# A second buffer for the gates' tile of two SwiGLU FFNs, with a smaller scratch for dynamic transfers

## The chip, the core and the metric

The kernel runs on one core of one Trainium2 chip. A core has a matrix engine (TensorE, PE in the profile; PEld is its loading of weights), three engines for elementwise work (VectorE or DVE, ScalarE or ACT, GpSimd or POOL) and SyncE (SP), which here only issues transfers. Operands lie in on-chip memory of 128 partitions (SBUF); TensorE writes its results to a second, small memory (PSUM), from where VectorE and ScalarE fetch them. Each engine has a list of instructions of its own and waits on semaphores for the others. The metric is the device time of one execution in microseconds (us).

## The reference, cut to what matters

Two layers of a transformer-like network work on 512 latent and 256 context tokens with a model width of 1024, in float32. Each layer has a mixer (attention and linear recurrences) and then an FFN:

```
def _swiglu(h, w_gate, w_up, w_down):
    return (jax.nn.silu(h @ w_gate) * (h @ w_up)) @ w_down
...
x_lat = x_lat + m_lat[5] * _rms(_swiglu(h_lat, ffn_w_gate[l], ffn_w_up[l], ffn_w_down[l]), norm_post_ffn[l])
```

The inner width is 2816, or 22 chunks of 128. Layer 0 (FFN 0) has 768 tokens, layer 1 (FFN 1) the 512 latent ones. The factors `m_lat` come from a product of a conditioning vector with `mod_w`, 6144 columns per layer.

## The kernel before, in words

Each float32 operand is split into a high part (H) and a low part (L) that TensorE multiplies fast, and a product is the sum of three matmuls HH, HL, LH. A weight block comes by a transfer on SP's queue into `raw` (three buffers); ScalarE copies its high part to `wH`, VectorE subtracts to get `wL` (L672 and L673 for whole units, L727 and L728 for the pairs below).

`ffn` works on the 22 chunks in pairs. For each pair it makes a *gate unit* (`product(wg, c0, "go", todo)`) and an *up unit* (`product(wu, c0, "uo")`), and between and behind them adds a part of the result of `w_down` (`acc_part`, PSUM tiles `acc`, sums into `y` on VectorE, L820). The first pair is done apart (`first`), so each FFN has ten gate units and ten up units with `product`.

A unit multiplies a 2 × 2 block matrix of weights with one of activations by Strassen's scheme, in `seven`: seven block products of 12 matmuls each instead of eight. With n = 384 (FFN 0) or 256 (FFN 1) columns per matmul, the blocks are, in program order, `11` (PSUM tile `ab`, first half), `U1` (`E`), `12` (`ab`, second half), `U2` (`ab`, first half again), `22` (`D`), `S4` (`E`) and `V` (`ab`). This text calls `22` block D, `U1` block E where it follows `11`, and keeps the names 11, 12, U2, V. In the rows of the profile and of the instruction lists, 11 is `ab<-b`, 12 is `ab<-x` with `wH` or `wL`, U2 is `ab<-T`, V is `ab<-x` with `dH` or `dL`.

The results go to an SBUF tile `X`, which is `go` for gate units and `uo` for up units, by eight small instructions: ScalarE's copies L791 (after 11), L793 (after U1), L801 (after U2), L803 (after 22) and VectorE's sums L799 (after 12), L806 (after S4), L808 and L809 (after V). Block 12 may write its half of `ab` only when L791 has read the other, U2 only when L799 is done, V when L801 is done.

After a gate unit ScalarE applies SiLU in place (L1572). After the up unit `gated` multiplies: `uo` = `uo` · `go` on VectorE (L1523, one instruction for each half k of the tokens), high part `gH` on ScalarE (L1525), low part `gL` on VectorE (L1526). This is put off to the next gate unit (`todo`, called by `seven` right after U1's copy): so a new `go` is begun while the old one is still to be read by L1523. The pool `fp` holds `go` and `uo` with one buffer each.

In FFN 0 a generator (`late_mods`, `mod_vec`) adds the products with `mod_w` as filler on VectorE (L530, tiles `macc`, fed by transfers to `mraw`). At the end of FFN 0 `go`, `uo` and `macc` are reused for weights of the next layer (`values`, tiles `ogo`, `ouo`, `oH`, `oL`).

The order of the instructions on each engine is not the order in which the code stands. In the FFNs a list scheduler sets it from priorities, from the buffers that are free and from its own estimates of durations; within an engine the order is then fixed. A tile that needs a buffer which is still in use has its first writer wait for the last reader of the old one.

Of the kernel before, what the change touches and what calls it, by code (L numbers as in the profile page):

```python
# [8 lines left out]
F32 = mybir.dt.float32  # L9
F32R = mybir.dt.float32r  # L10
# [7 lines left out]
P = 128  # L18
D = 1024
# [297 lines left out]
class Net:  # L317
# [1186 lines left out]
    def ffn(self, l, xp, yp, fp, pp, rp, h, ending, extra=None):  # L1504


        nc, I = self.nc, self.I
        wg, wu, wd = I["ffn_w_gate"][l], I["ffn_w_up"][l], I["ffn_w_down"][l]
        tiles, n = h.order, h.n
        extra = extra(fp) if extra else iter(())  # L1510
        fill = lambda *_: next(extra, None)
        singles = [(i,) for i in range(len(tiles))]

        gp = rp if l else fp

        def gu(x):
            return fp.tile([P, 2, 2 * n], F32, tag=x, bufs=1, name=x)

        def gated(pool, k, g, u, HL=None, mult=True):

            g, u = (x[:, :, n * k : n * k + n] for x in (g, u))
            if mult:
                nc.vector.tensor_tensor(u, u, g, op=ALU.mult)  # L1523
            H, L = HL or h.gated_tiles(pool, k)
            nc.scalar.copy(H, u)  # L1525
            nc.vector.tensor_tensor(L, u, H.bitcast(F32), op=ALU.subtract)  # L1526
            return H, L

        def first():

            cur = h.gated if l else [h.gated_tiles(gp, k) for k in range(2)]
            g, u = gu("go"), gu("uo")
            us = [[self.unit_cols(w, i * P) for w in (wg, wu)] for i in range(2)]
            h.open(xp)
            for half in range(2):
                pm = self.mm_tile("pearly")
                pts = [[self.sc_tile("pearly", x)[:, :n] for x in range(2)], [pm[:, 512 * x : 512 * x + n] for x in range(2)]]
                tok = slice(n * half, n * half + n)
                for ks in ((range(4), range(4, 8)) if half == 0 else (range(8),)):
                    for i in range(2):  # L1540
                        for m in range(2):
                            for k in ks:
                                self.mm3(pts[i][m], tuple(x[:, k, :] for x in us[i][m]), h.raw(k, half), k == 0, k == KD - 1)
                            if ks[0] == 0 and half == 0 and m == 0:
                                self.turn(1 - i)
                for i in range(2):
                    nc.scalar.activation(g[:, i, tok], pts[i][0], AF.Silu)
                    nc.vector.tensor_tensor(u[:, i, tok], g[:, i, tok], pts[i][1], op=ALU.mult)
                gated(gp, half, g, u, cur[half], False)
                if half == 0:  # L1550
                    pp.release()
                    tp = self.open_pool(f"t{l}")
                    h.sums(tp)
            h.late()
            return tp, cur

        def units(c0):
            return [self.rows_unit(wd, c0 + i) for i in range(2)]

        def product(w, c0, x, then=None):  # L1560
            x = gu(x)
            self.seven(self.pair_operands(tp, w, c0 * P, [tp] if l else [], 1 + l), h, x, fill if c0 > 2 else lambda: None, then)
            return x

        tp, cur = first()
        y = None
        todo = None
        for c0 in range(2, NFC, 2):
            g = product(wg, c0, "go", todo)
            for k in range(2):  # L1570
                x = g[:, :, n * k : n * k + n]
                nc.scalar.activation(x, x, AF.Silu)  # L1572
            if c0 + 2 < NFC:
                if y is None:
                    y = yp.tile([P, len(tiles), D], F32, tag="y", bufs=1, name=f"y{l}")
                self.acc_part([(units(c0 - 2), cur)], n, tiles, singles, y, c0 == 2, fill)
                u = product(wu, c0, "uo")
                cur = [h.gated_tiles(gp, k) for k in range(2)]

                def todo(g=g, u=u, cur=cur):  # L1580
                    for k in range(2):
                        gated(gp, k, g, u, cur[k], True)

            else:
                u = product(wu, c0, "uo")
        for _ in extra:
            pass
        tp.release()
        if gp is not rp:
            rp.release()  # L1590
        end, follow, pool = ending(y)

        last = [gated(pool, k, g, u) for k in range(2)]
        parts = [(units(c0 - 2), cur), (units(c0), last)]
        next(follow, None)
        self.acc_part(parts, n, tiles, [(0, 1)] + singles[2:], y, False, end)
        for left in (2, 1, 0):
            next(follow, None)
            self.turn(left)
        next(follow, None)  # L1600
        if gp is rp:
            rp.release()
        return y

    def run(self):
        nc, I, out = self.nc, self.I, self.out
# [10 lines left out]
        def xat(x):  # L1617
            return lambda t: x[t * P : (t + 1) * P, :]
# [108 lines left out]
        def ender(pp, l, m, tiles, xsrc, xdst, nxt, h=None):  # L1727

            if nxt is not None:
                nl, ns, nb, nrow = nxt  # L1730
            done = {}

            def gates():
                return {r: self.gate_row(pp, l, m, r) for r in ((0, 1) if len(tiles) > LT else (0,))}

            if (l, m) in self.gates:
                done["gv"] = gates()

            def end(y, t):
                if "nxt" not in done:  # L1740
                    if "gv" not in done:
                        done["gv"] = gates()
                    done["nxt"] = nxt and (self.affine(nl, ns, nrow, 1 if ns == 4 and nl else 2), self.mod_m(nl, nb), h)
                self.post_pre(pp, y, t, done["gv"], xsrc, xdst if xdst(t) is not None else None, done["nxt"], 2 if nxt is None and t == tiles[-1] else 1)

            return end

        def only_lat(f):
            return lambda t: f(t) if t < LT else None
# [18 lines left out]
        fp = self.open_pool("f0", "right")  # L1768
# [14 lines left out]
        def ending(ys):  # L1783
            ep = self.open_pool("e0b")

            def values():

                to = [[fp.tile([P, D], F32R, tag=x, bufs=1, name=f"o{x}") for x in ("go", "uo")]]
                to.append([fp.tile([P, D], F32R, tag="macc", bufs=2, name=f"o{x}") for x in "HL"])
                us = self.wide_units(3 * D, to)  # L1790
                yield
                self.odd_values(ys, h1, 0, (4,), us)
                yield
                yield
                self.odd_values(ys, h1, 0, (0,), us)
                yield
                self.odd_values(ys, h1, 0, (2,), us)
                ep.release()

            return ender(ep, 0, 5, order, xat(x1), only_lat(xat(x2)), (1, 1, 0, R_NPM), h1), values(), ep  # L1800
# [8 lines left out]
        fp = self.open_pool("f1", "right")  # L1809
# [68 lines left out]
```

## Time and profile before

| | us |
|---|---|
| three timed runs | 1738.44, 1744.97, 1744.47 (median 1744.47) |
| the profiled execution, its own time | 1732.31 |
| its span from the first to the last instruction | 1730.5 |
| TensorE busy in the span | 1681.9 |
| VectorE busy | 1288.3 |
| ScalarE busy | 863.7 |
| FFN 0, about | 430 to 910 |
| FFN 1, about | 1390 to 1705 |

Numbers in the text that look like 1587.73 are microseconds from the start of the span. A row of a timeline has the start, the duration, the engine, the line, the operation with its output and inputs, their shapes and a count; in brackets stands the idle time of the engine just before it and what ended it. A row of the waits has who waited, for whom, the total in us, how often, and the longest. A row of the chain has start, duration and what ran; the chain is followed back from the last instruction, at each step to what released it.

### The profile page before, as it was taken

Reading aid. Unit: us, or ns where it says so; the run is one execution under the profiler, and the core shown is the slowest. Engines: PE = TensorE matmul, PEld = TensorE weight load, DVE = VectorE, ACT = ScalarE, POOL = GpSimd, SP = SyncE. Lnnn points to the kernel's source line nnn. Section 1 sums busy time; section 2 is a strip of 40 time slices with the busy share of each in tenths; the row PEclk is TensorE's granted clock in tenths of the full one; section 3 lists DMA queues with packets and bytes.
Section 4 is the critical chain, followed back from the end, with each engine's and each line's share of the span. In section 5 each row is a group of like instructions: output and inputs, shape, how many; then the busy total and the mean of one; then the engine's idle time right before and its main releaser. Section 6 shows DMA issues by size and latency. Waiting matters only on the chain. (4 is left out here: it accounts for less than half of the span.)

```text
span 1730.5 us, 32414 instructions
## 1 busy us (share of the span) xinstructions
PE 1681.9 (97%) x13512; PEld 1506.6 (87%) x13512; DVE 1288.3 (74%) x2061; ACT 863.7 (50%) x1496; POOL 73.3 (4%) x93
## 2 busy tenths in 40 slices
PE   7999998999999999999999999999999999999998
PEld 5899987888998889898997888889888899999997
DVE  5889668836969999796668328787864678878785
ACT  4745568746442323233346436666644754444342
POOL 1004110000000000000001000000000000000000
PEclk9999999999999999999999999999999999999999
DMA  9641012144334465452225222121114333333333
GB/s 321 195 143 39 2 62 88 61 134 146 111 97 144 133 193 171 131 179 62 74 86 186 82 73 62 42 59 51 50 62 141 116 110 99 94 102 110 94 102 122
DMA packets 169838, 187.22 MB, mean 108 GB/s; under 512 B 6454, under 2 KB 141148, under 8 KB 169692
## 3 DMA queue, kind: packets, MB, share of 16 engines
q1 hardware_dynamic: 167760, 181.56, 33.1%
q10 hardware_dynamic: 1932, 3.59, 0.6%
q8 instruction: 106, 1.74, 0.4%
q14 instruction: 40, 0.33, 0.1%
HBM read 175.66 MB, written 9.46 MB: 107 GB/s over the span
## 5 line engine op out<-in xcount | busy, mean ns | idle before, releaser
L348 PE MATMUL nat<-wH,x 128*128 128x256 f32 (+2 forms) x944 | 216.2, 319 | 5.1 <-ACT x L641 2.6
L673 DVE TENSOR_TENSOR wL<-raw,wH 128x1024 fp32r<-128x1024 f32 (+1 forms) x126 | 151.0, 1207 | 91.8 <-ACT wH L672 91.3
L727 ACT CAST wH<-raw 128x1024 fp32r<-128x1024 f32 x120 | 124.6, 1052 | 175.7 <-PE acc L348 73.6
L728 DVE TENSOR_TENSOR wL<-raw,wH 128x1024 fp32r<-128x1024 f32 x120 | 145.3, 1221 | 62.3 <-ACT wH L727 62.2
L348 PEld LDWEIGHTS nat<-wH,x 128*128 128x128 f32 x944 | 157.6, 190 | 21.5 <-ACT x L641 3.6
L348 PE MATMUL acc<-wH,gH 128*128 128x512 f32 x440 | 172.6, 393 | 0.0
L672 ACT CAST wH<-raw 128x1024 fp32r<-128x1024 f32 (+1 forms) x126 | 129.0, 1040 | 85.9 <-PE nat L348 25.2
L348 PE MATMUL acc<-wH,gL 128*128 128x512 f32 x440 | 171.7, 390 | 0.0
L348 PE MATMUL acc<-wL,gH 128*128 128x512 f32 x440 | 171.6, 390 | 0.0
L348 PE MATMUL nat<-wL,x 128*128 128x256 f32 (+2 forms) x472 | 148.6, 315 | 0.0
L820 DVE TENSOR_TENSOR y<-y,acc 128x1024 f32<-128x1024 f32 x135 | 114.9, 863 | 32.2 <-PE acc L348 28.8
L348 PE MATMUL ff<-x,wH 128*128 128x512 f32 (+1 forms) x512 | 127.5, 340 | 0.0
L530 DVE SCALAR_TENSOR_TENSOR macc<-mraw,scT,macc 128x1024 f32<-128x1024 f32 x98 | 123.0, 1281 | 5.0 <-DMA mraw<-in_mod_w_dram 4.7
L600 POOL TENSOR_TENSOR rs<-ms,neghalf 128x1 f32<-128x1 f32 (+2 forms) x62 | 57.2, 924 | 1582.6 <-DVE ms L598 1582.5
L348 PE MATMUL oproj<-wH,x 128*128 128x512 f32 x320 | 101.6, 395 | 0.0
L348 PEld LDWEIGHTS acc<-wH,gH 128*128 128x128 f32 x440 | 82.6, 188 | 19.7 <-issue 1.7
L348 PEld LDWEIGHTS acc<-wH,gL 128*128 128x128 f32 x440 | 82.6, 188 | 17.3
L348 PEld LDWEIGHTS acc<-wL,gH 128*128 128x128 f32 x440 | 82.7, 188 | 16.1
L348 PEld LDWEIGHTS ff<-x,wH 128*128 128x128 f32 x512 | 87.4, 190 | 10.0
L348 PEld LDWEIGHTS nat<-wL,x 128*128 128x128 f32 x472 | 89.8, 190 | 5.1
L923 ACT COPY qkh<-arr 128x512 f32<-128x512 f32 x112 | 70.1, 642 | 36.3 <-DVE arr L928 32.1
L348 PE MATMUL ff<-x,wL 128*128 128x256 f32 (+1 forms) x256 | 86.1, 337 | 0.0
(344 smaller groups left out, 4045.5 us busy)
## 6 DMA issues: line engine op xcount, KB each, us to landing
mraw<-in_mod_w_dram SPq DMA_DIRECT2D x80, 512.0 KB, 3.8
raw<-in_ffn_w_gate_dram SPq DMA_DIRECT2D x44, 512.0 KB, 3.7
raw<-in_ffn_w_up_dram SPq DMA_DIRECT2D x44, 512.0 KB, 4.0
raw<-in_ffn_w_down_dram SPq DMA_DIRECT2D x44, 512.0 KB, 3.5
raw<-in_odd_w_in_dram SPq DMA_DIRECT2D x40, 512.0 KB, 3.8
mraw<-in_mod_w_dram SPq DMA_DIRECT2D x32, 256.0 KB, 6.1
raw<-in_even_w_in_dram SPq DMA_DIRECT2D x16, 512.0 KB, 3.7
x<-xr SPq DMA_DIRECT2D x14, 512.0 KB, 2.6
```

Source lines behind the costliest of these rows:

```text
L348: return self.pin(self.nc.tensor.matmul(*a, **k))
L530: nc.vector.scalar_tensor_tensor(a, u, w, a, op0=ALU.mult, op1=ALU.add)
L600: nc.gpsimd.tensor_tensor(rs, ms, self.neghalf.to_broadcast([P, w]), op=ALU.pow)
L672: nc.scalar.copy(H[:, :m], raw[:, :m])
L673: nc.vector.tensor_tensor(L[:, :m], raw[:, :m], H[:, :m].bitcast(F32), op=ALU.subtract)
L727: self.nc.scalar.copy(H, f)
L728: self.nc.vector.tensor_tensor(L, f, H.bitcast(F32), op=ALU.subtract)
L820: nc.vector.tensor_tensor(y, y, pt, op=ALU.add)
L923: nc.scalar.copy(qkv[:, :, :, half, :], dst)
```

## The change

The tile `go` gets two buffers in the pool `fp`, in both FFNs, at both places that name it; `uo` keeps one. The scratch that the program sets aside in SBUF for dynamic transfers, 16,384 bytes in each partition before, becomes 512 bytes. A `go` takes 6,144 bytes in each partition in FFN 0 and 4,096 in FFN 1.

```
@@ gu, in ffn
-            return fp.tile([P, 2, 2 * n], F32, tag=x, bufs=1, name=x)
+            return fp.tile([P, 2, 2 * n], F32, tag=x, bufs=2 if x == "go" else 1, name=x)
...
@@ values, in ending of FFN 0
-                to = [[fp.tile([P, D], F32R, tag=x, bufs=1, name=f"o{x}") for x in ("go", "uo")]]
+                to = [[fp.tile([P, D], F32R, tag=x, bufs=2 if x == "go" else 1, name=f"o{x}") for x in ("go", "uo")]]
...
@@ kernel
-    nc = bacc.Bacc("TRN2", target_bir_lowering=False, num_devices=1)
+    nc = bacc.Bacc("TRN2", target_bir_lowering=False, num_devices=1, dynamic_dma_scratch_size=512)
```

The number of instructions is the same on each engine, and so is all that they compute. The scheduler puts them in another order in the two FFNs; elsewhere the lists are the same. GpSimd's list does not change. Most tiles lie 15,872 bytes lower in SBUF.

On TensorE, in a gate unit of the middle of FFN 1, before (E is U1's tile, D that of 22, `ab<-x_14404` is block 12, `ab<-T_14566` is U2):

```order
L348 MATMUL E<-T_14565,wL 128x256
L348 MATMUL D<-x_14405,wH 128x256 x2
L348 MATMUL ab<-x_14404,wH 128x256 x2
...
L348 MATMUL ab<-x_14404,wL 128x256
L348 MATMUL D<-x_14405,wL 128x256
...
L348 MATMUL ab<-T_14566,wH 128x256 x2
```

and after:

```order
L348 MATMUL E<-T_14565,wL 128x256
L348 MATMUL ab<-x_14404,wH 128x256 x2
...
L348 MATMUL ab<-x_14404,wL 128x256
L348 MATMUL D<-x_14405,wH 128x256 x2
...
L348 MATMUL ab<-T_14566,wH 128x256 x2
```

Block 12 now follows U1 at once, where two matmuls of D stood between, and eleven matmuls of D stand between 12 and U2 where nine stood. On VectorE the list at this place is, before and after:

```order
L1523 TENSOR_TENSOR uo<-uo,go 128x2x256 x2
L673 TENSOR_TENSOR wL<-raw,wH 128x1024
L1526 TENSOR_TENSOR gL<-uo,gH 128x512 x2
L799 TENSOR_TENSOR go<-go,ab 128x256
L752 TENSOR_TENSOR ws<-raw 128x512
```

Nothing moved there. On ScalarE, in the third gate unit of FFN 0 (near 547 us before):

```order
 L727 COPY dH<-ws 128x512
-L727 COPY wH<-raw 128x1024
-L672 COPY wH<-raw 128x1024 x2
+L791 COPY go<-ab 128x384
+L727 COPY wH<-raw 128x1024
+L672 COPY wH<-raw 128x1024
+L793 COPY go<-E 128x384
+L1525 COPY gH<-uo 128x768
+L672 COPY wH<-raw 128x1024
+L1525 COPY gH<-uo 128x768
```

The copies into `go` and the first `gH` moved ahead of weight copies. On VectorE, at the same unit:

```order
+L1526 TENSOR_TENSOR gL<-uo,gH 128x768
 L530 TENSOR_SCALAR macc_6341<-mraw_6482,scT,macc_6341 128x1024
+L1526 TENSOR_TENSOR gL<-uo,gH 128x768
+L799 TENSOR_TENSOR go<-go,ab 128x384
 L530 TENSOR_SCALAR macc_6340<-mraw_6577,scT,macc_6340 128x1024
 L530 TENSOR_SCALAR macc_6341<-mraw_6577,scT,macc_6341 128x1024
-L1526 TENSOR_TENSOR gL<-uo,gH 128x768 x2
-L799 TENSOR_TENSOR go<-go,ab 128x384
```

L1526 and L799 moved ahead of one and of two of the sums L530.

## The prediction

> **What bounds the kernel now.** I read the page's engine table first, then the busy time by stretch, then TensorE's own waits in each FFN, then the chain that ended last, and last the timelines around single waits.
>
> ```profile
> span 1730.5 us, 32414 instructions
> PE 1681.9 (97%) x13512; PEld 1506.6 (87%) x13512; DVE 1288.3 (74%) x2061; ACT 863.7 (50%) x1496; POOL 73.3 (4%) x93
> ...
> 430.00:910.00 480.00, 474.86 (x2524) 437.41 (x2524) 395.47 (x483) 176.48 (x242) 0.00 (x0) 1.00 0.40 125
> 1390.00:1705.00 315.00, 310.19 (x2142) 288.34 (x2141) 248.27 (x349) 145.90 (x228) 0.00 (x0) 1.00 0.34 104
> ```
>
> The last two rows are the two FFNs (us, then busy time of PE, PEld, DVE, ACT, POOL, then clock). TensorE is the bound: it idles 480.00 − 474.86 = 5.1 us in FFN 0 and 315.00 − 310.19 = 4.8 us in FFN 1, at a granted clock of 1.00. The change moves nothing else, so some 10 us and the restarts behind each wait are all that it can win. Who ends those idle times (FFN 0's rows first, FFN 1's behind the dots):
>
> ```profile
> PE ab L348 <- DVE uo L799: 2.7, 3, 1.5
> PE ab L348 <- ACT go L791: 1.9, 2, 1.4
> PE ab L348 <- DVE go L799: 0.4, 1, 0.4
> ...
> PE ab L348 <- ACT go L791: 4.0, 8, 1.0
> PE ab L348 <- DVE uo L799: 0.7, 1, 0.7
> ...
> ACT go L791 <- DVE uo L1523: 43.3, 16, 3.3
> ```
>
> The copy L791 takes the first product (block 11) of a gate unit out of PSUM into `go`. By the last row, from the waits of the whole kernel, ScalarE stands still until VectorE's multiplication L1523 has read the old `go`: one buffer, so new values wait for old ones to be used. By the rows above, TensorE waits for that copy twice in FFN 0 and eight times in FFN 1: 5.9 us in all. This is what the second buffer addresses.
>
> But what else comes at that place? The chain that ended last, in one period of FFN 1 (start, us, what):
>
> ```profile
> 1574.48 2.28 DVE wL L728 x2
> ...
> 1576.78 4.75 DMA raw<-in_ffn_w_up_dram
> ...
> 1581.55 1.06 ACT wH L727
> ...
> 1584.19 1.14 DVE wL L673
> ...
> 1587.31 0.38 ACT go L791
> 1587.69 0.04 issue
> 1587.73 1.70 PE ab L348 x12
> 1589.43 1.08 PE D L348 x9
> 1590.51 1.44 PE ab L348 x12
> ```
>
> The chain enters TensorE at 1587.73 by way of VectorE and a weight load, not from TensorE's own last matmul. So in this loop of about 32 us a path DMA, ScalarE, VectorE is as long as TensorE's work, and every gate unit ends with TensorE waiting for it. The last row gives the price of a matmul with 256 columns: 1.44 / 12 = 0.12 us. VectorE and TensorE at the same place:
>
> ```profile
> 1585.91 1.29 DVE L1523 TENSOR_TENSOR uo<-uo,go 128x512 f32<-128x512 f32 x2
> 1587.11 1.22 DVE L673 TENSOR_TENSOR wL<-raw,wH 128x1024 fp32r<-128x1024 f32 x1
> 1588.50 1.29 DVE L1526 TENSOR_TENSOR gL<-uo,gH 128x512 fp32r<-128x512 f32 x2 [0.17 <-ACT gH L1525]
> 1589.71 0.42 DVE L799 TENSOR_TENSOR go<-go,ab 128x256 f32<-128x256 f32 x1
> ...
> 1586.80 0.40 PE L348 MATMUL D<-x,wH 128*128 128x256 f32 x2
> 1587.73 0.51 PE L348 MATMUL ab<-x,wH 128*128 128x256 f32 x2 [0.54 <-ACT go L791]
> 1590.35 0.40 PE L348 MATMUL ab<-T,wH 128*128 128x256 f32 x2
> ```
>
> The reader should see the four VectorE rows without a gap but for 0.17 us, and that L799 ends at 1589.71 + 0.42 = 1590.13, only 0.22 us before block U2 (`ab<-T`), which reads what L799 has made room for, starts at 1590.35.
>
> **The change, part by part.** *FFN 1, eight gate units.* L791 no longer waits for L1523: it can run when block 11 is done, under block E, which follows. TensorE's new order puts block 12 (`ab<-x`) straight behind E, where D stood, so it starts at 1586.80 instead of 1587.73. Then 12 and eleven of D take 23 × 0.12 = 2.76 us, and U2 could start at 1589.56: by TensorE alone the gain is 1590.35 − 1589.56 = 0.79 us (the wait of 0.54 and the slow restart behind it). VectorE does not allow that. Its order there is unchanged: L1523 twice, the weight part L673, L1526 twice, L799. Only the 0.17 us can go, since ScalarE makes `gH` sooner once its copies no longer wait. L673 ends at 1587.11 + 1.22 = 1588.33, L1526 starts there, L799 ends 0.17 us sooner at 1589.96, and with the 0.04 us between a release and its user in the chain, U2 starts at 1590.00. The gain is 0.35 us; the other 0.44 becomes a new wait of U2 for `go` L799. Eight units make 8 × 0.35 = 2.8 us. All of it shortens the period, since what follows U2, up to the load that starts the next round, keeps its order. The bounds: nothing, if L1526 does not move and U2 already follows L799 as fast as it can; 8 × 0.79 = 6.3 us, if VectorE's weight part finds another place. I take 2.8, since the rows show VectorE with no other slack.
>
> *FFN 0, gate units.* Here VectorE also sums the modulation (L530), and the lists of all three engines change. The largest wait:
>
> ```profile
> 551.79 0.96 DVE L1523 TENSOR_TENSOR uo<-uo,go 128x768 f32<-128x768 f32 x1
> 552.66 3.67 DVE L530 SCALAR_TENSOR_TENSOR macc<-mraw,scT,macc 128x1024 f32<-128x1024 f32 x3
> 557.98 0.56 DVE L799 TENSOR_TENSOR go<-go,ab 128x384 f32<-128x384 f32 x1
> ...
> 553.99 0.47 ACT L791 COPY go<-ab 128x384 f32<-128x384 f32 x1
> ...
> 554.51 0.62 PE L348 MATMUL ab<-x,wH 128*128 128x384 f32 x2 [1.38 <-ACT go L791]
> ```
>
> L791 stands behind two weight copies (L672) on ScalarE before; now it stands ahead of them. On VectorE L799 moves ahead of two of the three L530, 2 × 3.67 / 3 = 2.4 us sooner: it would start near 555.5 and end near 556.1. TensorE's new list has U2 behind 12 and nine of E (D, also ahead of it, was done before 12 in the old one): 554.51 − 1.53 + 21 × 0.18 = 556.8, with 0.18 as 1.5 × 0.12 for 384 columns. So here VectorE can follow, and the whole 1.38 us goes with 0.15 of restart (above: 0.93 between D's start and 12's, less two of D, less 0.54): 1.5 us. The second of the two waits (1.9 − 1.4 = 0.5 us) lies where VectorE is full; I take 0.3 of it. At one `uo` unit L799 moves ahead of a weight part, 1.2 us like the L673 above, which covers one of the three waits for `uo` L799: the smallest can be no more than (2.7 − 1.5) / 2 = 0.6, I take 0.4. The other two stay, since L799 there stands behind L530 and its load:
>
> ```profile
> 732.42 1.28 DVE L530 SCALAR_TENSOR_TENSOR macc<-mraw,scT,macc 128x1024 f32<-128x1024 f32 x1 [1.64 <-DMA mraw<-in_mod_w_dram]
> ```
>
> FFN 0 wins 2.2 us; its bounds are all its waits, 5.0 us, and a loss, if L530 comes to stand badly (a rival below).
>
> *The end of FFN 0.* `ogo`, weights for the next layer, takes a `go` buffer and now needn't wait. ScalarE's list has its copy (L672) ahead of the last `wH`:
>
> ```profile
> 906.98 0.48 ACT L803 ACTIVATE uo<-D 128x384 f32<-128x384 f32 x1
> 908.11 1.05 ACT L672 CAST wH<-raw 128x1024 fp32r<-128x1024 f32 x1 [0.64 <-ACT uo L803]
> 912.25 1.70 ACT L1525 CAST gH<-uo 128x768 fp32r<-128x768 f32 x2 [3.09 <-DVE uo L1523]
> ```
>
> Behind it are queued this `wH`, VectorE's `wL`, then L808, L809, L1523 and the last `gH`. From 907.46 the 0.64 us of idle time takes part of a copy of 1.05, so `gH` comes 0.4 us later, more if the weights land late. TensorE has 24 matmuls of older operands before it needs `gH`, which began at 910.12 (two tiles, two halves, two weight units, three matmuls each): about 5.5 us at the 0.23 between these two rows, to 915.6, and `gH`'s first half is ready near 913. Cost nothing; without that cover 1.05 us at most.
>
> ```profile
> 910.12 0.39 PE L348 MATMUL acc<-wH,gH 128*128 128x512 f32 x1
> 910.35 0.40 PE L348 MATMUL acc<-wL,gH 128*128 128x512 f32 x1
> ```
>
> *SP, GpSimd, addresses.* GpSimd's list is the same. On SP two gate loads each move ahead of one modulation load, and a modulation load ahead of a `w_down` load, in a stretch where TensorE has no wait named above but those of 0.6 and 1.5: nothing, or one 1.64 as above. Most tiles lie 15,872 bytes lower: no row prices that; I take nothing.
>
> The sum is 2.8 + 2.2 = 5.0 us: 1732.3 for the profiled execution (span 1730.5 and 1.8 around it) becomes 1727.3. That execution lies 12.2 us under the median, 1744.5, as a whole; the difference carries over, and I forecast 1744.5 − 5.0 = 1739.5 us.
>
> **The rivals.** *A: all the waits go.* If VectorE's weight part no longer stands in the way, because the earlier `gH` and loads shift that list, FFN 1 wins 6.3 and FFN 0 its 5.0: 1744.5 − 11.3 = 1733.2. For it: the same gap of half a microsecond stands in each of eight units, with one cause. Against it: the VectorE rows above. The Trainium skill, page Perfetto Trace Analysis, section Optimization Strategy, says that one gap that repeats on the engine that should be busy can mean too few buffers for the next tile; by that rule this is the case to expect. The trace agrees on the gap, but shows the next releaser 0.22 us behind.
>
> *B: the wait only moves.* U2 then waits for L799 at the old time in FFN 1, and full VectorE takes the gain back in FFN 0, where 58.34 of 60 us are busy:
>
> ```profile
> 540.00:600.00 60.00, 58.62 (x316) 53.92 (x315) 58.34 (x71) 17.56 (x25) 0.00 (x0) 1.00 0.47 148
> ```
>
> About 1743.5. For it speaks the unchanged list; against it the 0.17 and the slack.
>
> *C: slower, by L530 in FFN 0.* Its modulation weights have few buffers; L530 that slips behind its load stops VectorE for 1.64 us (row at 732.42), and L799 and TensorE behind it. Six products of FFN 0 are reordered. From four such slips on (6.6 us) it outweighs the gain; six would cost 9.8 − 5.0 = +4.8: 1749.3.
>
> *D: slower, by the small scratch.* If the transfers needed it, each weight load would land later. The load of 4.75 us lies on the chain, so each us is paid in full: from 0.63 us on, eight periods (5.0) eat the gain; a doubled landing costs 8 × 4.75 = 38 us there alone, 1777 with the gain. Against it: the transfers are of one kind.
>
> ```profile
> q1 hardware_dynamic: 167760, 181.56, 33.1%
> q10 hardware_dynamic: 1932, 3.59, 0.6%
> ```
>
> The Trainium skill, page SBUF — State Buffer, section SBUF size: 192, 224, or 256?, takes this reserve for the ring of descriptors of transfers generated in software; by that, D costs nothing, and the trace names only hardware queues. No run here has shown the scratch's size matter either way.
>
> **How the numbers follow.** Forecast 0.38 (own range 1734 to 1744), A 0.30, B 0.12, C 0.12, D 0.08. 0.5% is 8.7 us, about what a measurement of this kernel can tell from no change, and the three runs themselves span 6.5. Faster by more (under 1735.8): most of A, 0.25, and the low third of the forecast, 0.12: 0.37. Slower by more (over 1753.2): D and half of C, 0.16 with a little of B. Within: 0.47. The range goes from A's 1733.2 less half the runs' span, 1730, to C's 1749.3, 1750.
>
> **What would show it.** In the waits of TensorE `ab <- ACT go L791` is gone and `ab <- DVE go L799` has come, near 0.4 us in eight gate units. ScalarE's 43.3 us of waiting for `uo` L1523 before `go` shrinks and moves to `gH`. U2 in FFN 1 starts within 0.1 us of L799's end, and the period drops by 0.3 to 0.4 us. If it drops by 0.7, A holds; if loads land later than 4.75 us there, D. New idle time of VectorE before L530 in FFN 0 would be C.

## The result and the profile after

| | before | after |
|---|---|---|
| median of fifteen runs, us | 1738.5 | 1735.7 |
| lowest to highest, us | 1734.7 to 1745.0 | 1732.9 to 1737.5 |
| ratio of after to before | | 0.9977 (95% interval 0.9966 to 0.9987) |
| span of the profiled execution, us | 1730.5 | 1734.3 |

The change makes the kernel faster by 0.23%, or 4.0 us of 1738.5, with an interval from 2.3 to 5.9 us (the medians differ by 2.8 us, the means, 1739.5 and 1735.3, by 4.1). The same kernel, timed again beside other runs, gave 0.9970 (0.9958 to 0.9981). The forecast was a gain of 5.0 us.

The two profiled executions stand the other way round: the one of after is 3.8 us longer. They can't be subtracted as wholes. The busy time by stretch shows one reason, between the FFNs, first before, then after (us, busy time of PE, PEld, DVE, ACT, POOL, the granted clock, share and rate of the transfers):

```profile
1300.00:1390.00 90.00, 87.67 (x513) 76.04 (x513) 55.38 (x70) 52.04 (x93) 5.41 (x9) 1.00 0.37 123
```

```profile
430.00:910.00 480.00, 473.48 (x2514) 435.74 (x2513) 394.04 (x481) 176.91 (x242) 0.00 (x0) 1.00 0.41 125
1300.00:1390.00 90.00, 87.32 (x490) 75.34 (x489) 52.49 (x66) 52.11 (x92) 5.42 (x9) 0.98 0.38 123
1390.00:1705.00 315.00, 310.22 (x2158) 289.03 (x2157) 246.81 (x347) 145.66 (x226) 0.00 (x0) 1.00 0.35 102
```

In the stretch ahead of FFN 1, which the change does not touch, the clock granted to TensorE was 0.98 after and 1.00 before; 2% of 90 us are 1.8 us. From the start of FFN 0's tenth gate unit to that of FFN 1's first it took 512.4 us after and 510.5 before. In both FFNs the clock was 1.00. So I compare within the FFNs. TensorE's waits there, FFN 0 first and FFN 1 behind the dots:

```profile
PE ab L348 <- DVE go L799: 2.5, 4, 1.0
PE ab L348 <- DVE uo L799: 2.3, 3, 1.1
PE ab L348 <- ACT go L791: 0.6, 1, 0.6
...
PE ab L348 <- DVE go L799: 2.9, 7, 1.0
PE ab L348 <- ACT uo L791: 1.0, 1, 1.0
PE ab L348 <- DVE uo L799: 0.7, 1, 0.7
...
ACT go L791 <- PE ab L348: 18.3, 17, 1.6
```

Of the ten waits for `go` L791 one of 0.6 us is left. In FFN 1 seven waits of U2 for `go` L799 have come, 2.9 / 7 = 0.4 us each, and one of 1.0 us for `uo` L791, which lies in the first period. By the last row, from the waits of the whole kernel, ScalarE's L791 now waits for block 11 itself and no longer 43.3 us for VectorE's L1523. VectorE and then TensorE in one gate unit of FFN 1:

```profile
1590.58 1.28 DVE L1523 TENSOR_TENSOR uo<-uo,go 128x512 f32<-128x512 f32 x2
1591.78 1.22 DVE L673 TENSOR_TENSOR wL<-raw,wH 128x1024 fp32r<-128x1024 f32 x1
1592.92 1.28 DVE L1526 TENSOR_TENSOR gL<-uo,gH 128x512 fp32r<-128x512 f32 x2
1594.12 0.41 DVE L799 TENSOR_TENSOR go<-go,ab 128x256 f32<-128x256 f32 x1
...
1594.59 0.50 PE L348 MATMUL ab<-T,wH 128*128 128x256 f32 x2 [0.36 <-DVE go L799]
```

The 0.17 us ahead of L1526 is gone, VectorE's four rows follow each other without a gap, and U2 starts 0.06 us behind L799. From the start of L1523 to that of U2 it is 1594.59 − 1590.58 = 4.01 us, where before it was 1590.35 − 1585.91 = 4.44: 0.43 us less in this unit. The chain that ended last goes through the same four rows, and through something more:

```profile
1579.00 2.28 DVE wL L728 x2
...
1581.30 4.90 DMA raw<-in_ffn_w_up_dram
...
1586.22 1.06 ACT wH L727
...
1591.86 1.14 DVE wL L673
1593.00 1.20 DVE gL L1526 x2
1594.20 0.34 DVE go L799
...
1594.59 1.70 PE ab L348 x12
```

The loop of FFN 1 is closed as before: the load of `w_up` waits for L728, VectorE's list waits for the load, TensorE for VectorE's list. Here the load took 4.90 us, against 4.75 at that place before.

To measure the FFNs across runs I take the time from the start of block 11 of the first gate unit to that of the tenth (nine periods, called the *way* below), from the timeline rows of `ab<-b`. For FFN 1 after, the first and the last of them:

```profile
1395.02 0.40 PE L348 MATMUL ab<-b,wH 128*128 128x256 f32 x2
...
1683.93 0.40 PE L348 MATMUL ab<-b,wH 128*128 128x256 f32 x2
```

That is 288.91 us after, and it was 288.80 before; in FFN 0 429.62 after and 427.80 before. By this pair of executions nothing is won. How far one execution can be trusted is the first thing that the experiments had to show.

### The profile page after: what moved, and what is told of

Read it like the earlier page. It is cut to its first block, busy times and chain, and to the rows that moved or that the text cites. A ratio compares the mean times of both kernels' runs of the same rounds, so it can differ in the third digit from the quotient of the medians.

```text
span 1734.3 us, 32373 instructions
## 1 busy us (share of the span) xinstructions
PE 1682.6 (97%) x13512; PEld 1507.3 (87%) x13512; DVE 1287.2 (74%) x2061; ACT 865.9 (50%) x1496; POOL 73.6 (4%) x93
## 5 line engine op out<-in xcount | busy, mean ns | idle before, releaser
L673 DVE TENSOR_TENSOR wL<-raw,wH 128x1024 fp32r<-128x1024 f32 (+1 forms) x126 | 150.9, 1205 | 91.8 <-ACT wH L672 91.2
L728 DVE TENSOR_TENSOR wL<-raw,wH 128x1024 fp32r<-128x1024 f32 x120 | 145.0, 1220 | 63.9 <-ACT wH L727 63.9
L530 DVE SCALAR_TENSOR_TENSOR macc<-mraw,scT,macc 128x1024 f32<-128x1024 f32 x98 | 123.0, 1277 | 7.3 <-DMA mraw<-in_mod_w_dram 7.1
```

The source lines that it names most:

```text
L530: nc.vector.scalar_tensor_tensor(a, u, w, a, op0=ALU.mult, op1=ALU.add)
L673: nc.vector.tensor_tensor(L[:, :m], raw[:, :m], H[:, :m].bitcast(F32), op=ALU.subtract)
L728: self.nc.vector.tensor_tensor(L, f, H.bitcast(F32), op=ALU.subtract)
```

## The experiments

The runs are described below, one by one. All are timed against the kernel before on the same chip. The way is that of one profiled execution each; the last column holds the last six periods of FFN 1.

| run | ratio (95% interval) | way of FFN 0 | way of FFN 1 | its last six periods |
|---|---|---|---|---|
| before | 1 | 427.80 | 288.80 | 192.20 |
| after | 0.9977 (0.9966 to 0.9987) | 429.62 | 288.91 | 191.15 |
| again | 0.9970 (0.9958 to 0.9981) | 426.55 | 287.48 | 190.50 |
| scratch | 0.9991 (0.9981 to 1.0002) | 428.20 | 289.02 | 191.93 |
| ffn1 | 0.9984 (0.9975 to 0.9993) | 430.53 | 288.92 | 191.66 |
| ffn1_big | 0.9977 (0.9966 to 0.9988) | 427.93 | 286.09 | 189.81 |
| ffn0 | 0.9996 (0.9986 to 1.0006) | 429.70 | 292.17 | 193.72 |
| late | 1.0016 (1.0002 to 1.0030) | 424.60 | 297.89 | 199.94 |
| pool1 | 1.0139 (1.0121 to 1.0158) | 429.78 | 318.45 | 212.98 |
| raw4_go1 | 0.9977 (0.9967 to 0.9987) | 425.95 | 288.71 | 190.63 |
| raw4 | 0.9957 (0.9943 to 0.9971) | 425.64 | 287.24 | 189.94 |
| mraw3 | 0.9956 (0.9939 to 0.9972) | 425.24 | 286.95 | 189.72 |
| raw4_late0 | 0.9949 (0.9936 to 0.9961) | 423.99 | 288.00 | 190.22 |
| raw4_late | 0.9946 (0.9933 to 0.9959) | 423.53 | 288.38 | 190.35 |

**The parts of the change.** Run `scratch` is the kernel before with the small scratch alone:

```
-    nc = bacc.Bacc("TRN2", target_bir_lowering=False, num_devices=1)
+    nc = bacc.Bacc("TRN2", target_bir_lowering=False, num_devices=1, dynamic_dma_scratch_size=512)
```

> Only the small scratch; `go` keeps one buffer, so every list is that of before and only addresses differ. Theory S (the two FFN gains of the prediction, the scratch does nothing): ratio 1.000 within its interval, `ab <- ACT go L791` back at 5 to 6 us over both FFNs, the up load on the chain of FFN 1 at 4.7 to 4.8 us as before. Rival D (the small scratch delays loads: in the changed kernel's profile that load took 4.90 and 4.94 us on the chain, against 4.75 before): the load takes 4.9 us here too, and the kernel is 1 to 1.5 us slower than before, ratio 1.0006 to 1.001.

Runs `ffn1` and `ffn0` are the kernel after with the second buffer in one FFN only, and `again` is the kernel after itself:

```
-            return fp.tile([P, 2, 2 * n], F32, tag=x, bufs=2 if x == "go" else 1, name=x)
+            return fp.tile([P, 2, 2 * n], F32, tag=x, bufs=2 if x == "go" and l else 1, name=x)
...
+            return fp.tile([P, 2, 2 * n], F32, tag=x, bufs=2 if x == "go" and not l else 1, name=x)
```

In `ffn1` the weights that reuse `go` behind FFN 0 have one buffer too. In `before`, `after`, `scratch`, these two and `ffn1_big` below, the lists of VectorE and ScalarE in an FFN hang on its number of `go` buffers alone; where that is the same, they are the same.

> The small scratch and the second `go` buffer in FFN 1 alone; FFN 0 is as before. Theory S as predicted: -2.8 us, ratio 0.9984, a period 0.35 us shorter. What the changed kernel's profile says (six periods of FFN 1 from 192.2 to 191.2 us, U2 waiting 0.2 to 0.4 us for L799): about -1 to -1.5 us, ratio 0.9992. Rival B (the wait only moves): 1.000.

> The small scratch and the second `go` buffer in FFN 0 alone (and for the weights that reuse it); FFN 1 is as before. Theory S: -2.2 us, ratio 0.9987. Rival C (sums of the modulation come to stand badly; in the changed kernel's one profile the fourth to fifth gate unit took 2.2 us longer than before, the whole of FFN 0 1.7): +1.7 us, ratio 1.001. If most of the gain is here: -3 to -4 us, 0.998.

> The changed kernel itself once more, for a second profile beside these. Ratio 0.9977 within about 0.001, and the sum of the parts: its gain is that of ffn1 and ffn0 together less what scratch costs. If FFN 0's loss of 1.7 us in the first profile was one execution's transfers, it is not here; if it is rival C, it is.

FFN 1 carries the gain: 0.9984 (2.8 us) with FFN 1 alone, 0.9996 (0.7 us, not clear of zero) with FFN 0 alone, 0.9991 (1.6 us, not clear of zero) with the scratch alone. Each has an interval of about 1.7 us to either side, so these parts needn't add up; the 2.2 us forecast for FFN 0 lie just within its interval, and a loss of 1.7 us, the other expectation, outside. The waits of the run `scratch`, FFN 0 and then FFN 1, show that L791 is waited for as before:

```profile
PE ab L348 <- ACT go L791: 1.9, 2, 1.4
...
PE ab L348 <- ACT go L791: 4.2, 8, 1.2
```

Whether the 1.6 us of `scratch` were its own was tried from the other side, in the run `ffn1_big`. FFN 1 leaves enough memory free for the second buffer without making the scratch smaller:

```
-    nc = bacc.Bacc("TRN2", target_bir_lowering=False, num_devices=1, dynamic_dma_scratch_size=512)
+    nc = bacc.Bacc("TRN2", target_bir_lowering=False, num_devices=1)
```

> The second `go` buffer in FFN 1 alone, with the scratch of before (in FFN 1 the space is there). If the scratch has no effect: the ratio of the run with the small scratch, 0.9984, within 0.001, and TensorE's lost time in FFN 1 near 9.5 us as in the other profiles with two buffers there. If the 1.6 us of the run with the scratch alone (0.9991) were the scratch's doing: only 0.9993, some 1.2 us under before.

0.9977, as good as the whole change. So the scratch's size adds nothing that these runs can tell, in either direction, and rival D falls. The long `w_up` loads of the first profile (4.90 us) don't come with the small scratch: in `scratch` those on the chain from 1515 to 1644 us took 4.3 to 4.7 us, and in `again`, from 1515 on, 4.7 to 4.8.

Now the profiles can be used together. With one `go` buffer in FFN 1 its way is 288.80, 289.02 and 292.17 (mean 290.0), with two 288.91, 287.48, 288.92 and 286.09 (mean 287.9): 2.1 us. In the last six periods the means are 192.62 and 190.78, which is 0.31 us per period, but single executions of the same lists differ by 1.8 us there. The stretch that the change acts on is much steadier than the period. From the start of L1523 to that of U2, in the six units ahead of the last, it takes 4.42 to 4.44 us in all three profiles with one buffer, and 4.00 to 4.01 in those with two (4.16 and 4.19 in two units of `ffn1_big`). So the second buffer wins 0.43 us in a gate unit of FFN 1. The rest of the period is 27.5 to 27.8 us with either number; most of the difference between executions of one kernel comes from there.

In FFN 0, four profiles have one buffer (427.80, 428.20, 430.53, 427.93, mean 428.6) and four have two (429.62, 429.70, 426.55 and that of `pool1`, 429.78, mean 428.9): by the ways alone nothing is won there. The loss of 1.8 us in the first pair of profiles is not there in `again` (426.55). Kernels with the same lists in an FFN differ by 3 us from one execution to the next.

**Where the gain of FFN 0 went.** The largest of FFN 0's waits did go. ScalarE, VectorE and TensorE in the third gate unit after, one view each:

```profile
549.13 0.48 ACT L791 COPY go<-ab 128x384 f32<-128x384 f32 x1 [1.58 <-PE ab L348]
```

```profile
555.86 0.55 DVE L799 TENSOR_TENSOR go<-go,ab 128x384 f32<-128x384 f32 x1
```

```profile
551.01 0.51 PE L348 MATMUL ab<-x,wH 128*128 128x384 f32 x2
...
556.73 0.51 PE L348 MATMUL ab<-T,wH 128*128 128x384 f32 x2
```

U2 starts at 556.73 without a wait, where the prediction had 556.8. From the last matmul of block 11 in this unit to that in the next it takes 47.86, 47.83, 47.85 and 47.84 us in the four profiles with two buffers, and 49.11, 49.15, 49.09 and 49.08 in those with one: 1.25 us won, each time. (The starts of block 11 can't be compared there: in the new order two matmuls of the fourth unit's block 11 run ahead of V.) Other periods give it back, in part or wholly. By the same count the fourth takes 0.2 us more on average, where a wait for L791 of 0.6 us is left (0.5 before). The ninth takes 46.35, 46.73, 46.25 and 46.40 against 45.91, 46.12, 46.27 and 46.07, a mean of 0.3 us more, and the fifth 48.65, 47.12, 45.77 and 48.31 against 46.49, 45.79, 48.17 and 45.81, a mean of 0.9 more with a wide spread. In the fifth, in the profile after, VectorE and then TensorE:

```profile
643.13 1.28 DVE L530 SCALAR_TENSOR_TENSOR macc<-mraw,scT,macc 128x1024 f32<-128x1024 f32 x1 [1.83 <-DMA mraw<-in_mod_w_dram]
...
655.01 0.55 DVE L799 TENSOR_TENSOR go<-go,ab 128x384 f32<-128x384 f32 x1
...
655.61 0.62 PE L348 MATMUL ab<-T,wH 128*128 128x384 f32 x2 [1.00 <-DVE go L799]
```

VectorE stood still for a modulation load at 643, its list had no other slack up to 655, and U2 paid. That is rival C's mechanism, at a smaller price. The run `mraw3` tried it with a third buffer for `mraw`:

```
-    def mod_vec(self, pool, jobs, own=None, bufs=2, sums=2):
+    def mod_vec(self, pool, jobs, own=None, bufs=3, sums=2):
...
-        tmp = self.wp.tile([P, WU], F32, tag="mraw", bufs=2, name="pn")
+        tmp = self.wp.tile([P, WU], F32, tag="mraw", bufs=3, name="pn")
```

and the same for the other tiles that share the tag.

> The changed kernel with three buffers instead of two for `mraw`, the tile of the modulation weights (it is shared with other short-lived tiles, so the order shifts a little elsewhere too). Rival C (VectorE's sums L530, waiting for their loads, eat what the second `go` buffer wins in FFN 0): L530's waits for `mraw` in FFN 0 (7.0, 6.9, 3.8 and 6.9 us in four profiles with the second buffer there) fall under 3, the way from the first to the last gate unit of FFN 0 falls from 429 to about 427, and the ratio from 0.9974 to about 0.996. If VectorE's own work is what is full there (rival B), the waits fall but the way stays at 428.5 to 429.5 and the ratio at 0.997 to 0.998.

VectorE's waits for these loads in FFN 0, in the kernel after, in the same kernel again, and then in `mraw3`:

```profile
DVE macc L530 <- DMA mraw<-in_mod_w_dram: 7.0, 6, 1.8
```

```profile
DVE macc L530 <- DMA mraw<-in_mod_w_dram: 3.8, 6, 1.0
```

```profile
DVE macc L530 <- DMA mraw<-in_mod_w_dram: 0.5, 1, 0.5
```

In `mraw3` the waits fall from 7.0 to 0.5 us, the way of FFN 0 from a mean of 428.9 to 425.2, and the ratio to 0.9956. The scheduler also put VectorE's and ScalarE's lists of FFN 0 in another order there, so this run alone can't say that it was the loads. The executions of unchanged lists say more. With one `go` buffer the waits are 4.7, 4.3, 7.2 and 4.3 us, beside ways of 427.80, 428.20, 430.53 and 427.93; with two they are 7.0, 6.9, 3.8 and 6.9, beside 429.62, 429.70, 426.55 and 429.78. The way follows the waits almost us for us, so in these executions L530's loads do bound FFN 0, and they make most of the 3 us between them. Less these waits the ways are 423.1 to 423.9 (mean 423.5) with one buffer and 422.6 to 422.9 (mean 422.8) with two. That is an estimate of 0.7 us for what the second buffer wins in FFN 0 when the loads land alike, the same as the run `ffn0` gave, though that was not clear of zero. That the reordering made the loads' waits longer is not shown, and a third `mraw` buffer with a single `go` wasn't tried.

**What comes next in FFN 1: VectorE's list.** In the run `late`, L1526 is made behind L799:

```
@@ seven
-                        then()
+                        lows = then()
...
-                nc.vector.tensor_tensor(c11, c11, pt, op=ALU.add)
+                with self.tc.issue_after(nc.vector.tensor_tensor(c11, c11, pt, op=ALU.add).ins): [low() for low in lows]
@@ gated, in ffn
-            nc.vector.tensor_tensor(L, u, H.bitcast(F32), op=ALU.subtract)
-            return H, L
+            low = lambda: nc.vector.tensor_tensor(L, u, H.bitcast(F32), op=ALU.subtract)
+            return low if put_off else (low(), (H, L))[1]
```

> The changed kernel with one step moved: the two low parts of the product (L1526, 1.2 us for both in FFN 1) are made behind VectorE's sum L799 instead of ahead of it, in both FFNs. Theory V (VectorE's list between L1523 and L799 is the next bound): L799 ends 1.2 us sooner, ahead of the end of eleven matmuls of D, so U2's waits for `go` L799 in FFN 1 (2.9 and 1.8 us in the two profiles) fall under 0.3, the last six periods from 191.15 and 190.50 to about 188.5, and the kernel gains another 2.5 to 3.5 us: ratio to before 0.9955. Rival L (the loop of FFN 1 goes through the late load of `w_up` and the wait only shows up elsewhere): the waits for L799 go, others of the same size come, the six periods stay at 190.5 to 191.2, ratio 0.997 as for the changed kernel. In FFN 0 either says little: within 1.5 us.

FFN 1 became 10 us longer than the mean of the kernels with two `go` buffers, which neither theory had. VectorE in one gate unit:

```profile
1590.95 1.22 DVE L673 TENSOR_TENSOR wL<-raw,wH 128x1024 fp32r<-128x1024 f32 x1
1593.12 0.69 DVE L752 TENSOR_TENSOR ws<-raw 128x512 f32<-128x512 f32 x1 [0.96 <-DMA raw<-in_ffn_w_up_dram]
1593.73 0.41 DVE L799 TENSOR_TENSOR go<-go,ab 128x256 f32<-128x256 f32 x1
```

The scheduler put L752, the first sum of the next unit's weights, ahead of L799, and L752 waits for the load of `w_up`. VectorE runs its list in order, so L799 waits with it: U2's waits for `go` L799 come to 10.3 us. In FFN 0, where the same edit brought no such wait, the way fell to 424.6.

`pool1` takes the other instruction, L673 of `w_down`, off VectorE's list in FFN 1 and gives it to GpSimd:

```
@@ unit
-        nc.vector.tensor_tensor(L[:, :m], raw[:, :m], H[:, :m].bitcast(F32), op=ALU.subtract)
+        (low or nc.vector).tensor_tensor(L[:, :m], raw[:, :m], H[:, :m].bitcast(F32), op=ALU.subtract)
@@ units, in ffn
-            return [self.rows_unit(wd, c0 + i) for i in range(2)]
+            return [self.rows_unit(wd, c0 + i, low=nc.gpsimd if l else None) for i in range(2)]
```

> The changed kernel, with the low parts of `w_down` in FFN 1 (L673, two of 1.14 us per period) subtracted by GpSimd instead of VectorE. Theory V: L799 comes 0.5 to 1.1 us sooner, the waits for it in FFN 1 go as in the run above, 2.5 to 3.5 us, ratio 0.9955. Rival L: 0.997. If GpSimd is slow or the two engines disturb each other (no row of before has GpSimd at this shape), `acc` waits for `wL` in FFN 1 and the kernel is slower than the changed one, 0.999 or above.

The third outcome came, far more strongly than expected: 1.0139, with a way of FFN 1 some 30 us longer than in the kernel after. Not `acc` waits, but VectorE. The groups by line in the steady part of FFN 1 (count, busy us, mean ns of one):

```profile
L673 POOL TENSOR_TENSOR wL<-raw,wH 128x1024 fp32r<-128x1024 f32 x12 | 31.3, 2632 | 181.7 <-DVE wL L728 121.2 <-PE ab L348 60.6
L1523 DVE TENSOR_TENSOR uo<-uo,go 128x512 f32<-128x512 f32 x12 | 28.7, 2427 | 0.0
...
L1526 DVE TENSOR_TENSOR gL<-uo,gH 128x512 fp32r<-128x512 f32 x12 | 7.7, 684 | 0.0
```

L1523, which takes 681 ns in the kernel after, takes 2427 ns, because it runs beside the subtraction on GpSimd (the last section has the rows). U2's waits for `go` L799 in FFN 1 grow to 22.1 us with it, so nothing is learnt here on theory V.

**What comes next in FFN 1: the load.** `raw4` gives `raw` four buffers, and `raw4_go1` does the same with a single `go` buffer:

```
-        raw = self.wp.tile([P, WU], F32, tag="raw", bufs=3, name="raw")
+        raw = self.wp.tile([P, WU], F32, tag="raw", bufs=4, name="raw")
```

and so for the three other places with that tag.

> The changed kernel with four buffers for `raw` instead of three, everywhere. Rival L: the load of `w_up` is issued without waiting for L728, so VectorE's L808 and L1523, which came 1.5 us behind the end of V, come up to 1.5 us sooner; the waits for L799 go and the first periods lose less; FFN 1 gains 3 to 5 us, FFN 0 1 to 3 (its waits for `uo` L799): ratio 0.9925 to 0.995. Theory V: VectorE's list holds as before, the gain stays under 1 us: 0.9970.

> The kernel before with the small scratch and four `raw` buffers; `go` has one. If the late load was the root (rival L), L1523 comes so early that L791 needn't wait even with one buffer: `ab <- ACT go L791` in FFN 1 falls from 4.0 to under 1 us and the ratio is that of the run above within 0.001. If the second buffer counts by itself, the waits for L791 stay at 3 us or more and it is 2 to 3 us slower than the run above.

The load mostly leaves the loop. The chain of `raw4` in one gate unit of FFN 1 enters VectorE from TensorE's block V, by way of a weight copy (`dH`):

```profile
1551.15 1.33 PE ab L348 x11
...
1552.51 0.63 ACT dH L727
...
1553.16 0.41 DVE uo L808
...
1555.11 1.14 DVE wL L673
1556.24 0.60 DVE raw L752
...
1557.36 0.68 DVE gL L1526
1558.05 0.34 DVE go L799
...
1558.43 1.69 PE ab L348 x12
```

There is no transfer in this part of the chain any more, and still U2 starts behind L799, at the end of a list in which VectorE has no gap. Both theories have their half. In the last six periods of FFN 1 one load of `w_up` is left on the chain of `raw4`, where the kernel after has five. The six periods put a price on the two edits. With one `go` and three `raw` buffers they take 192.62 (mean of three), with a second `go` 190.78 (mean of four), with a fourth `raw` 190.63 (one execution), with both 189.94 (in `raw4_late0` below, where FFN 1 is as in `raw4`, 190.22). Either edit alone wins about 1.9 us there, and the second to come only 0.4 to 0.8: both take slack from the same loop. That rests on few executions, which differ by as much as this second gain, and the timed runs don't show it: of the whole kernel the second `go` wins 4.0 us, the fourth `raw` (with the small scratch) 4.0 and both 7.5, each with an interval of about 2 us to either side. With one `go` the waits for L791 stay, 3.0 us in FFN 1, and `raw4_go1` is 3.5 us slower than `raw4`, so the second buffer counts by itself, as the second of the expectations said, with a little more than its 2 to 3 us. The 3 to 5 us that rival L expected of FFN 1 did not come. Most of what the fourth buffer wins lies in FFN 0, 3.3 us against the mean of the kernel after.

Last, the fourth buffer with L1526 moved, in both FFNs (`raw4_late`) and in FFN 0 alone (`raw4_late0`, where the flag is `not l`):

```
-                    return [gated(gp, k, g, u, cur[k], True, True) for k in range(2)]
+                    return [gated(gp, k, g, u, cur[k], True, not l) for k in range(2)]
```

> Four `raw` buffers, two `go` buffers, and the low parts L1526 behind L799 in both FFNs. In the run that moved L1526 with three `raw` buffers, VectorE stood 0.96 us for a load ahead of L799 in FFN 1; with four the instruction ahead of it reads a tile that has landed before. Theory V+L (load and list are both bounds of the loop in FFN 1): waits of U2 for L799 under 0.5 us in all, FFN 1 another 1 to 1.5 us shorter than with four `raw` buffers alone, FFN 0 0 to 1 shorter: ratio 0.9945 to 0.995. If only the load was the bound: 0.9957 as with four `raw` buffers alone. If another load comes to stand ahead of L799: 0.998 or worse, with VectorE's wait in the rows.

> As the last run, but L1526 is moved behind L799 in FFN 0 alone. FFN 0's part of the last run by itself: 0 to 1 us under four `raw` buffers alone, ratio 0.9950 to 0.9957; FFN 1 as with four `raw` buffers alone (TensorE's lost time there 8.1 us, waits of U2 for L799 1.9).

These are the fastest of all: 0.9946 (median 1727.9 us) and 0.9949 (1728.9 us), 9 us under the kernel before. FFN 0 won more than the 0 to 1 us expected, 1.7 and 2.1 us under `raw4`. FFN 1 won nothing by the move: its way is 288.38 with it, and 287.24 (`raw4`) and 288.00 (`raw4_late0`) without, and U2's waits for `go` L799 are 3.0 us, not under 0.5. So the ratio of `raw4_late` lies where theory V+L had it, but by luck: what was to come from FFN 1 came from FFN 0. In FFN 1 theory V is thus not confirmed in its simple form: when L1526 goes out of the way, other instructions (L752, and L728 on `dH`) take its place ahead of L799 in the scheduler's list:

```profile
1551.00 1.22 DVE L673 TENSOR_TENSOR wL<-raw,wH 128x1024 fp32r<-128x1024 f32 x1
1552.13 0.68 DVE L752 TENSOR_TENSOR raw<-raw 128x512 f32<-128x512 f32 x1
1552.73 0.68 DVE L728 TENSOR_TENSOR dL<-ws,dH 128x512 fp32r<-128x512 f32 x1
1553.34 0.41 DVE L799 TENSOR_TENSOR go<-go,ab 128x256 f32<-128x256 f32 x1
```

## Why the prediction was right, and where it was not

- *The sign and the size.* A gain of 5.0 us was forecast; 4.0 (2.3 to 5.9) was measured. Its two parts did not come as worked out: FFN 1 won 0.43 us in a unit where 0.35 were forecast, and FFN 0 an estimated 0.7 us of 2.2. That the total fits so well is in part luck. The absolute time, 1735.7, lies 3.8 under the forecast of 1739.5. The median of three runs that the forecast started from, 1744.5, was 6.0 above that of fifteen, and the medians fell by 2.8 instead of 5.0.
- *FFN 1, eight units at 0.35 us.* Right in mechanism: the wait for L791 went, the 0.17 us ahead of L1526 went, U2 follows L799 within 0.06 us, and the new waits are 0.4 us, all as worked out. In each unit 0.43 us were won between L1523 and U2, not 0.35, since the working let L1526 start at the end of L673, 1588.33, and VectorE's rows overlap: without the gap L1526 starts 0.08 us ahead of that end (1592.92 beside 1591.78 + 1.22 = 1593.00). Eight units at 0.43 us would be 3.4 us. The way shows 2.1 and the periods 0.31 us each, with differences of 3 us between executions. One execution would have misled: in the profile after a period is only 0.17 us shorter (192.20 to 191.15), while its loads of `w_up` on the chain took up to 4.94 us instead of 4.75 and the loop is closed through them.
- *Rival A (all waits go).* It did not happen, for the reason given: VectorE's list stands 0.4 us behind. The gap that repeats did point to the right tile, but not to what the buffer is worth.
- *FFN 0, the wait of 1.38 us.* The step was right where it was worked out: U2 at 556.73 against 556.8, and 1.25 of the 1.5 us won in that period in every profile. The term as a whole, 2.2 us, failed: FFN 0's way did not fall (428.6 with one buffer, 428.9 with two), and with the load waits taken off it is 0.7 us shorter. The step that failed is the sum over FFN 0 as if each wait removed were time won, with L530 held to its place. What the runs show in its place is a way that goes with VectorE's waits for the modulation loads, 3.8 to 7.2 us in each execution, and later periods that lose again part of what the third wins. Whether the new order causes that loss stays open.
- *The smaller terms in FFN 0* (0.3 and 0.4 us). The first did not come: the second wait for L791 is still there, 0.6 us against 0.5. The other can't be told from executions that differ by 3 us.
- *Rival B.* Not in FFN 1. In FFN 0 its outcome nearly came, but not where it said: the 1.25 us were won in the very stretch where VectorE is full, and lost in later ones.
- *Rival C.* Its mechanism bounds FFN 0, with one buffer as with two; its price of 9.8 us did not come.
- *Rival D and the moved addresses.* Nothing, as taken: 0.9991 (0.9981 to 1.0002) with the scratch alone, 0.9977 with the old scratch and the buffer in FFN 1. (Besides the two hardware queues that the prediction shows, the page of the profile lists two of kind instruction, 2.07 MB in all.) The Trainium skill's account of the scratch (SBUF — State Buffer, section SBUF size: 192, 224, or 256?) agrees with these runs.
- *The end of FFN 0, costed at nothing.* From the tenth gate unit's start to the last `acc` matmul it took 67.5 us before and 67.4 after. Right.

## What to carry to other kernels

Before giving a tile a second buffer, find what releases the consumer next: here the wait that repeated in each unit was worth 0.79 us by TensorE alone, with its restart, and VectorE's list left 0.43 of it. When a path goes round a loop (a load, a copy, a sum, the matrix engine), don't add up two edits that each loosen it: a second `go` and a fourth `raw` buffer won 1.9 us each in the last six periods of FFN 1 and some 2.5 together, by few executions. A difference of a few us should be read in the stretch that the change touches, from its first wait to the next engine's start, and over several profiled executions: 0.43 us stood out there in each one, while the whole of an unchanged FFN differs by 3 us from one execution to the next. And the memory that a change frees may be worth more elsewhere, as a third `mraw` buffer and a fourth `raw` buffer were.

## What the runs showed of the hardware that was not expected

An instruction of VectorE can stand still for the whole of one on GpSimd. In the run `pool1` the two L673 on GpSimd ran from 1572.94 to 1578.16, and the two L1523 beside them ended 0.55 us behind the end of each:

```profile
1573.10 0.41 DVE L808 TENSOR_TENSOR uo<-uo,ab 128x256 f32<-128x256 f32 x1
1573.43 0.42 DVE L809 SCALAR_TENSOR_TENSOR uo<-ab,uo 128x256 f32<-128x256 f32 x1
1573.77 4.95 DVE L1523 TENSOR_TENSOR uo<-uo,go 128x512 f32<-128x512 f32 x2
...
1572.94 5.22 POOL L673 TENSOR_TENSOR wL<-raw,wH 128x1024 fp32r<-128x1024 f32 x2 [30.99 <-PE ab L348]
```

L808 and L809, which read one operand from PSUM, kept their 0.41 us in the same stretch; L1523 reads both from SBUF. At 1608 us the same pair stands in another place and again ends 0.55 us behind. The Trainium skill, page SBUF — State Buffer, section Who interferes with whom, says just that: a VectorE instruction with two SBUF inputs shares a read port with GpSimd, and the one that comes second is blocked until the other is done. The trace agrees, with 2.43 us for an instruction of 0.68. The subtraction itself took 2.63 us on GpSimd and 1.22 on VectorE.

The time from issue to landing of the same 512 KB load of `w_up` in the steady part of FFN 1 was 4.7 us (median) with three `raw` buffers and 4.0 with four, where SP issues it at another point of the period. Why it lands sooner there was not tried.
